# Reordering VectorE and ScalarE work around the fp32 feed-forward matmuls of a two-layer decoder trunk

## The chip, the cores and the metric

The kernel runs on one core of a Trainium2 chip. Its engines are TensorE (PE in the rows, its weight loads PEld), VectorE (DVE), ScalarE (ACT), GpSimd (POOL) and the DMA queue of SyncE (SP). The metric is the device time of one execution in microseconds (us); lower is better. The profile is that of one execution, and "span" is the time from its first to its last instruction.

## The reference

One step of a two-layer decoder trunk over 576 tokens (512 prompt tokens, 64 sample tokens), all in float32. Four SwiGLU feed-forward blocks stand around two mixers:

```python
def rms_norm(x, g):
    xf = x.astype(F32)
    y = xf * lax.rsqrt(jnp.mean(xf * xf, axis=-1, keepdims=True) + EPS)
    return (y * g.astype(F32)).astype(x.dtype)

def swiglu(x, w_gu, w_down):
    g, u = jnp.split(x @ w_gu, 2, axis=-1)
    return (jax.nn.silu(g) * u) @ w_down
...
    for l in range(DEPTH):
        x = x + 0.5 * swiglu(rms_norm(x, ffn1_norm[l]), ffn1_w_gu[l], ffn1_w_down[l])
        h = rms_norm(x, mix_norm[l])
...
        x = x + mix
        x = x + 0.5 * swiglu(rms_norm(x, ffn2_norm[l]), ffn2_w_gu[l], ffn2_w_down[l])
    y = rms_norm(x, final_norm)
```

The model width is 1024 and the hidden width 2816. The mixer of layer 0 is windowed attention with pooling, that of layer 1 a gated width-3 convolution; the change leaves both alone.

## The kernel before, in words

**Numbers.** Every float32 operand of a matmul is split into a high and a low part (`wh`, `wl` for weights; `xh`, `xl`, `exh`, `exl`, `hh`, `hl` for data), and three matmuls (high by high, high by low, low by high) make one product. The high part of a weight is a cast on ACT (L100), the low part a subtraction on DVE (L101). A weight tile has three buffers of each. `W.ahead(n)` issues the splits of the next weight groups, `W.take()` hands out the next one.

**Phases.** FFN 0, attention mixer, FFN 1, FFN 2, convolution, FFN 3, final norm. An FFN goes through the 22 hidden blocks in four chunks of 5, 5, 6 and 6; after a chunk's blocks come its eight down-projections, in the order 0, 4, 1, 5, 2, 6, 3, 7. The last chunk's projections add into x, prepare the next phase's operands from x and add x squared into `sq` (ACT squares into `sqt`, POOL adds, L298).

**A unit.** A hidden block's gate and up product is made with seven block products instead of eight, each a run of 12 matmuls of 128x128 by 128x288 (the tokens are two halves of C = 288). PE issues them in the order B11, T1, B21, T2, B22, T3, and T4 last. They go into three PSUM banks: A (B11, B21: gate of the first half), F (T1, B22: gate of the second half) and B (T2, T3, T4: up). Between them stand copies on ACT: A into B after B11 (L447), F into `p5` after T1 (L472), B into `u2` after T2 (L484). T3 adds to B and so waits for the copy into `u2`; B21 adds to A and waits for the copy of A into B; T4 adds to B and waits until DVE has read B for the *half sum* (h <- B + p5, L399). The gate's first half is multiplied by the norm factor on DVE (L431) and goes through Silu on ACT (L432); the second half is L435, L436, L437.

The weights of a unit are three groups: `a` straight from the loaded tile (`raw`), `e` and `f` from three *weight sums* on DVE (L111 to L113), and `dh`, `dl` for T4. T4 of a unit runs behind B11 of the next (`finish_unit`), because its half sum and split come late. The first unit of a chunk has no unit before it: it runs through the last part of `unit()`, the other units through the part under `if prev:`, which has an order of its own. Of the 16 first units, three (those that begin FFN 1, 2 and 3, `start`) also make the norm factor: column sums of `sq` on PE (L339), a square root on ACT (L343), a refinement on DVE, then transposes on PE (L358), copies into `r` on ACT (L623) and `rm` on DVE. The first three blocks of FFN 0 are done plainly (`first_pairs`), eight products each, while x is still being prepared. The program keeps each engine's order as written; semaphores join the engines.

Of the kernel before, what the change touches and what calls it, by code (L numbers as in the profile page):

```python
# [25 lines left out]
F32 = mybir.dt.float32  # L26
F32R = mybir.dt.float32r
AF = mybir.ActivationFunctionType
ALU = mybir.AluOpType
# [3 lines left out]
C = 288  # L33
# [6 lines left out]
PLAIN = 3  # L40
# [132 lines left out]
class Trunk:  # L173
    def __init__(self, ctx, tc, I, O, phases):
        self.tc, self.nc, self.I, self.O = tc, tc.nc, I, O
        nc = self.nc
# [18 lines left out]
        for ph in phases:  # L195
            if ph[0] == "ffn":
                n = ph[1]
# [4 lines left out]
            elif ph[0] == "ab":  # L202
                g = lambda ap: ap.rearrange("p a b -> p (a b)")
# [6 lines left out]
                units += [(f(I["cvo"][u]), 2048, (1024, 1024)) for u in range(4)]  # L210
        self.W = Weights(nc, self.raw_pool, self.split_pool, units)
        self.phases = phases

    def bank(self, n):
        return self.ps.tile([128, 512], F32, tag=n, name=n, bufs=2 if n == "B" else 3)
# [169 lines left out]
    def seven(self, out, name, w, col, first, last):  # L385
# [3 lines left out]
        for k in range(4):  # L389
            v = slice(col + 128 * k, col + 128 * k + 128)  # L390
            fh, fl = self.form(name, k)
            for z, (a, m) in enumerate(((h, fh), (h, fl), (l, fh))):
                nc.tensor.matmul(out=out, lhsT=a[:, v], rhs=m, start=(first and k == 0 and z == 0),  # L393
                                 stop=(last and k == 3 and z == 2), skip_group_check=True)

    def half_mult(self, s):

        nc, tt = self.nc, self.nc.vector.tensor_tensor
        tt(out=s["h"][:, C:], in0=s["B"][:, :C], in1=s["p5"], op=ALU.add)  # L399
        tt(out=s["h"][:, C:], in0=s["h"][:, C:], in1=s["g"][:, C:], op=ALU.mult)  # L400

    def finish_unit(self, s):

# [12 lines left out]
    def unit(self, u, j, prev, fresh, start, pre, extra=None):  # L416
# [13 lines left out]
        def gate0():  # L430
            tt(out=g0, in0=a, in1=r[:, :C], op=ALU.mult)  # L431
            nc.scalar.activation(out=g0, in_=g0, func=AF.Silu)  # L432
# [15 lines left out]
        if prev:  # L448
# [17 lines left out]
            nc.scalar.activation(out=g1, in_=g1, func=AF.Silu)  # L466
            self.seven(b, "T3", wf, 0, False, False)
            return s
        W.sums(u + 1)
        we = W.take()  # L470
        self.seven(f, "T1", we, 0, True, False)
        nc.scalar.copy(out=s["p5"], in_=f)  # L472
# [1 line left out]
        self.seven(a, "B21", wa, 512, False, True)  # L474
        if not start:
            gate0()
        W.ahead(1)
        if extra:
            extra()
# [9 lines left out]
            ft = self.factor_tiles()  # L489
        else:  # L490
            gate1()
        W.ahead(1)
        self.seven(b, "T3", wf, 0, False, False)
        if start:
            self.factor([fp[j // 4][:, 128 * (j % 4):128 * (j % 4) + v.stop - v.start] for j, v in enumerate(TOKS)], ft)
            gate0()
            gate1()
        return s


# [28 lines left out]
    def first_pairs(self, n):  # L529
        nc, W, tp = self.nc, self.W, self.tp  # L530
        ws = [W.take() for _ in range(2)]
        p0 = [self.pair() for _ in range(2)]
        for k in range(KD):
            for p, w in zip(p0, ws):
                self.eight(p, w, k, 128 * k, k == 0, k == 7)
        sq = [self.sq] + self.sqs
        for i, j in ((0, 1), (2, 3), (0, 2), (4, 5), (6, 7), (4, 6), (0, 4)):
            nc.vector.tensor_tensor(out=sq[i], in0=sq[i], in1=sq[j], op=ALU.add)
        self.hidden_tiles()
        W.ahead(1)  # L540
        for ks in ((0, 1), (2, 3)):
            ts = []
            for k in ks:
                ts.append(tp.tile([128, C], F32, tag="t1", name="t1"))
                nc.vector.tensor_tensor(out=ts[-1], in0=self.x[:, k, :C], in1=self.x[:, k, C:], op=ALU.subtract)
            for k, t in zip(ks, ts):
                self.hi_lo(self.form("T1", k), t, self.gain[:, n, k:k + 1])

        def sums(ks):
            sts = []  # L550
            for k in ks:
                xb = tp.tile([128, C], F32, tag="t1", name="t1")
                nc.scalar.activation(out=xb, in_=self.x[:, k, C:], func=AF.Copy, scale=self.gain[:, n, k:k + 1])
                sts.append((k, xb, tp.tile([128, 3, C], F32, tag="st", name="st")[:, :2]))
            for k, xb, st in sts:
                self.form_t32(k, n, xb, st)
            for k, xb, st in sts:
                self.main_hi(k, st)
            for k, xb, st in sts:
                self.main_lo(k, st)  # L560

        (g0, g1), (u0, u1) = p0
        pg = self.plain(self.pair())
        W.ahead(1)
        outs = [t[:, C:C + 128] for t in (g0, g1, u0, u1)] + [g0[:, 416:480]]
        fa, ft = [], []

        def roots():
            fa.append(self.tok_factor(g1[:, 480:485], (self.sq,), TOKS, later=True))

        def factors():
            self.newton(*fa[0])
            self.factor(outs, self.factor_tiles())

        pu = self.plain((self.bank("B"), self.bank("B")), {1: roots, 5: factors})
        self.plain_out(0, *p0)
        W.ahead(1)
        sums((0, 1))
        p2 = [self.plain(self.pair())]
        self.plain_out(1, pg, pu)  # L580
        W.sums(PLAIN)
        W.ahead(1)
        sums((2, 3))
        p2.append(self.plain(self.pair()))
        W.ahead(1)
        self.plain_out(2, *p2)

    def late_forms(self, n):

# [36 lines left out]
    def ffn(self, i, u0):  # L626
# [4 lines left out]
        for ci, (o, kc) in enumerate(CHUNKS):  # L631
# [17 lines left out]
            held = []  # L649
            for e, d in enumerate(ORDER):  # L650
                if last and kind == "final" and e == 6:
                    self.last_down(kc)
                    break
                w = self.W.next(1 if e == 1 else 2)
                p = self.pair()
                held.append((d, p, w))
                self.down_part(p, w, 0, kc - 1 if e < 2 else kc, kc)
# [4 lines left out]
                if e == 1:  # L662
                    for d, p, w in held:
                        self.down_part(p, w, kc - 1, 1, kc)
                    self.W.ahead(2)
                for d, p, w in held:
                    self.down_out(d, p, last, nxt, kind)
                held = []

    def down_out(self, d, p, last, nxt, kind):  # L670
        nc, tp, tt = self.nc, self.tp, self.nc.vector.tensor_tensor
# [13 lines left out]
            nc.scalar.activation(out=self.xg(d), in_=xd, func=AF.Copy, scale=self.gain[:, 6, d:d + 1])  # L685
        else:
            self.split_x(d, nxt)
        self.square(d, tp)

    def forms(self, d, nxt, tp):  # L690
        if d < 4:
# [899 lines left out]
```

## Time and profile before

| | |
|---|---|
| median of 3 runs | 2321.95 us (2320.99 to 2324.97) |
| the profiled execution's own time | 2320.83 us |
| its span | 2319.0 us |
| PE busy | 2216.7 us, 96% of the span |
| DVE busy | 1627.6 us, 70% |
| ACT busy | 925.3 us, 40% |
| POOL busy | 436.7 us, 19% |
| mean granted TensorE clock | 0.986 |
| share of the DMA engines, loads and stores of SP | 27.8% |

A matmul's busy time is longer than the step from one to the next, since they overlap; the pace is read from their starts. The engines work in parallel, so a busy share alone does not tell what a shorter wait is worth: that is read from PE's pauses and from what ended them.

### The profile page before, as it was taken

To read this page: it belongs to the slowest core of one execution; us is meant where nothing else is said; L and a number is where in the kernel's file an instruction comes from. 1 tells how busy PE (TensorE), PEld (TensorE's weight loads), DVE (VectorE), ACT (ScalarE), POOL (GpSimd) and SP (SyncE) were. 2 spreads that over 40 slices of the span, in tenths; PEclk is the share of its full clock that TensorE was granted. 3 is DMA by queue.
4 is the path that set the end of the run, shared out by engine and by line. 5 is a ranking of instruction groups with operands and counts; after the bars stand their busy time and mean duration, and the time that the engine had idled before them with its cause. 6 is when DMAs were issued, how large, how long until landed. Compare 5 with 4: busy or idle time off the path is not lost. (4 is left out here: it accounts for less than half of the span.)

```text
span 2319.0 us, 39839 instructions
## 1 busy us (share of the span) xinstructions
PE 2216.7 (96%) x16544; PEld 2167.9 (93%) x16544; DVE 1627.6 (70%) x2596; ACT 925.3 (40%) x1604; POOL 436.7 (19%) x444
## 2 busy tenths in 40 slices
PE   8899999999999999999999899999999999999998
PEld 7899999899888899999999899999999999999997
DVE  7586767635666788668587867768664487768584
ACT  5343534323334335344344524344431145335253
POOL 0000101207555640000011101000222211000012
PEclk9899999999999999999999899999999999999999
DMA  3222222443343522222222222322222222222222
GB/s 134 72 77 90 96 87 78 156 140 117 128 140 108 135 87 78 96 83 92 91 76 89 66 84 76 103 91 78 87 93 84 82 70 75 103 82 87 80 98 69
DMA packets 70949, 217.89 MB, mean 94 GB/s; under 512 B 14256, under 2 KB 37808, under 8 KB 54128
## 3 DMA queue, kind: packets, MB, share of 16 engines
q1 hardware_dynamic: 70336, 215.24, 27.8%
q8 instruction: 130, 2.13, 0.4%
q14 instruction: 51, 0.42, 0.1%
q10 hardware_dynamic: 432, 0.10, 0.0%
HBM read 204.22 MB, written 11.10 MB: 93 GB/s over the span
## 5 line engine op out<-in xcount | busy, mean ns | idle before, releaser
L101 DVE TENSOR_TENSOR wl<-raw,wh 128x1024 fp32r<-128x1024 f32 (+3 forms) x305 | 350.7, 1155 | 220.5 <-ACT wh L100 220.3
L100 ACT CAST wh<-raw 128x1024 fp32r<-128x1024 f32 (+3 forms) x305 | 278.1, 914 | 336.6 <-PE F L610 212.3
L414 POOL TENSOR_TENSOR hl<-h,hh 128x576 fp32r<-128x576 f32 x88 | 135.1, 1535 | 1378.8 <-ACT hh L413 1378.8
L393 PE MATMUL B<-xh,wh 128*128 128x288 f32 x680 | 203.1, 299 | 25.8 <-ACT u L484 25.8
L101 DVE TENSOR_TENSOR wl<-sum,wh 128x1024 fp32r<-128x1024 f32 x168 | 206.6, 1230 | 29.6 <-ACT wh L100 29.6
L393 PE MATMUL A<-exh,wh 128*128 128x288 f32 x680 | 204.4, 301 | 7.3 <-ACT B L447 7.1
L100 ACT CAST wh<-sum 128x1024 fp32r<-128x1024 f32 x168 | 174.0, 1047 | 93.4 <-DVE sum L112 92.0
L374 PE MATMUL acc<-xh,wh 128*128 128x288 f32 x960 | 207.7, 298 | 1.7 <-DVE x L681 1.7
L393 PE MATMUL A<-exh,wl 128*128 128x288 f32 x680 | 204.0, 300 | 3.9 <-DVE wl L101 3.9
L374 PE MATMUL acc<-xl,wh 128*128 128x288 f32 x960 | 205.6, 296 | 0.4 <-POOL xl L1441 0.4
L374 PE MATMUL acc<-xh,wl 128*128 128x288 f32 x960 | 205.6, 296 | 0.0
L610 PE MATMUL F<-hh,wh 128*128 128x288 f32 x692 | 205.5, 297 | 0.0
L610 PE MATMUL F<-hl,wh 128*128 128x288 f32 x692 | 205.4, 297 | 0.0
L610 PE MATMUL F<-hh,wl 128*128 128x288 f32 x692 | 205.3, 297 | 0.0
L610 PE MATMUL A<-hh,wl 128*128 128x288 f32 x692 | 204.0, 295 | 1.1 <-DVE wl L101 1.0
L610 PE MATMUL A<-hl,wh 128*128 128x288 f32 x692 | 203.9, 295 | 0.0
L610 PE MATMUL A<-hh,wh 128*128 128x288 f32 x692 | 203.8, 295 | 0.0
L393 PE MATMUL A<-exl,wh 128*128 128x288 f32 x680 | 203.8, 300 | 0.0
L393 PE MATMUL B<-xl,wh 128*128 128x288 f32 x680 | 201.6, 296 | 0.0
L393 PE MATMUL B<-xh,wl 128*128 128x288 f32 x680 | 201.5, 296 | 0.0
L374 PEld LDWEIGHTS acc<-xh,wh 128*128 128x128 f32 x960 | 154.3, 189 | 6.1 <-issue 3.2
L393 PEld LDWEIGHTS B<-xh,wh 128*128 128x128 f32 x680 | 128.9, 189 | 29.2 <-ACT u L484 29.2
(375 smaller groups left out, 6006.8 us busy)
## 6 DMA issues: line engine op xcount, KB each, us to landing
raw<-in_gu SPq DMA_DIRECT2D x87, 1024.0 KB, 4.9
raw<-in_dn SPq DMA_DIRECT2D x32, 768.0 KB, 4.3
raw<-in_dn SPq DMA_DIRECT2D x32, 640.0 KB, 3.9
raw<-in_wqk SPq DMA_DIRECT2D x12, 1024.0 KB, 5.2
raw<-in_cv SPq DMA_DIRECT2D x12, 1024.0 KB, 4.8
kv<-in_kb SPq DMA_DIRECT2D x32, 256.0 KB, 4.2
kv<-in_vb SPq DMA_DIRECT2D x32, 256.0 KB, 4.6
raw<-in_wv SPq DMA_DIRECT2D x6, 1024.0 KB, 4.8
```

The source lines that it names most:

```text
L100: self.nc.scalar.copy(out=h, in_=src)
L101: self.nc.vector.tensor_tensor(out=l, in0=src, in1=h.bitcast(F32), op=ALU.subtract)
L374: nc.tensor.matmul(out=p[:, c, :C], lhsT=w, rhs=m[:, k0 + k, c * C:c * C + C], start=(first and k == 0 and z == 0), stop=(last and k == kn ...
L393: nc.tensor.matmul(out=out, lhsT=a[:, v], rhs=m, start=(first and k == 0 and z == 0), stop=(last and k == 3 and z == 2), skip_group_check= ...
L414: nc.gpsimd.tensor_tensor(out=self.hl[:, j, :], in0=s["h"], in1=self.hh[:, j, :].bitcast(F32), op=ALU.subtract)
L610: nc.tensor.matmul(out=p[c][:, :C], lhsT=a, rhs=m[:, k, c * C:c * C + C], start=(k == 0 and z == 0), stop=(k == kc - 1 and z == 2))
```

## The change

Five orders are written differently; no operation is added or taken away.

1. In a first unit, the weight sums of the next unit (`W.sums(u + 1)`) no longer stand ahead of everything: they come behind the gate product `gate0`, or, in the three units that begin an FFN, behind T3's half sum.
2. The half sum of a first unit comes right behind T3's matmuls, and the split of the next weight group (`W.ahead(1)`) behind it; `half_mult` at the next unit then has nothing left to do.
3. In the units that begin an FFN, the sums and that split stand between the half sum and the copies into `r`.
4. In the last chunk of an FFN, the square of one x block is issued behind the next weight cast.
5. In `first_pairs`, splits of weights are issued earlier, the differences of x halves later, the first sums ahead of the factor copies, and the factor's two steps one k step earlier.

```diff
+    def half_add(self, s):
+
+        if "sum" not in s:
+            s["sum"] = True
+            self.nc.vector.tensor_tensor(out=s["h"][:, C:], in0=s["B"], in1=s["p5"], op=ALU.add)
+
     def half_mult(self, s):
-
-        nc, tt = self.nc, self.nc.vector.tensor_tensor
-        tt(out=s["h"][:, C:], in0=s["B"][:, :C], in1=s["p5"], op=ALU.add)
-        tt(out=s["h"][:, C:], in0=s["h"][:, C:], in1=s["g"][:, C:], op=ALU.mult)
+        self.half_add(s)
+        if "half" not in s:
+            s["half"] = True
+            self.nc.vector.tensor_tensor(out=s["h"][:, C:], in0=s["h"][:, C:], in1=s["g"][:, C:], op=ALU.mult)
...
-        W.sums(u + 1)
         we = W.take()
...
         if not start:
             gate0()
+            W.sums(u + 1)
         W.ahead(1)
...
             gate1()
-        W.ahead(1)
         self.seven(b, "T3", wf, 0, False, False)
+        self.half_add(s)
         if start:
+            W.sums(u + 1)
+            W.ahead(1)
             self.factor([fp[j // 4][:, 128 * (j % 4):128 * (j % 4) + v.stop - v.start] for j, v in enumerate(TOKS)], ft)
             gate0()
             gate1()
+            self.half_mult(s)
+        else:
+            self.half_mult(s)
+            W.ahead(1)
         return s
...
-        W.ahead(1)
-        for ks in ((0, 1), (2, 3)):
...
+        W.ahead(2)
+
+        def differences():
...
         pg = self.plain(self.pair())
-        W.ahead(1)
+        W.ahead(2)
...
         def factors():
             self.newton(*fa[0])
-            self.factor(outs, self.factor_tiles())
-
-        pu = self.plain((self.bank("B"), self.bank("B")), {1: roots, 5: factors})
+            ft = self.factor_tiles()
+            sums((0, 1))
+            self.factor(outs, ft)
+
+        pu = self.plain((self.bank("B"), self.bank("B")), {0: roots, 4: factors})
+        W.ahead(1)
         self.plain_out(0, *p0)
-        W.ahead(1)
-        sums((0, 1))
+        differences()
         p2 = [self.plain(self.pair())]
+        W.sums(PLAIN)
         self.plain_out(1, pg, pu)
-        W.sums(PLAIN)
-        W.ahead(1)
+        W.ahead(2)
         sums((2, 3))
         p2.append(self.plain(self.pair()))
+        self.plain_out(2, *p2)
         W.ahead(1)
-        self.plain_out(2, *p2)
...
                 w = self.W.next(1 if e == 1 else 2)
+                if self.late_square:
+                    self.late_square()
+                    self.late_square = None
                 p = self.pair()
...
-        self.square(d, tp)
+        self.late_square = lambda: self.square(d, tp)
```

PE's order differs at the two factor steps of `first_pairs` alone, and the orders of POOL and SP are the same in both programs. Three places of the other two engines follow.

DVE, first unit of the second chunk of FFN 0 (a first unit that begins no FFN); `wl<-sum` are the groups e and f, `wl<-raw` is the next unit's group a. Before:

```order
L101 TENSOR_TENSOR wl<-sum,wh 128x1024
L111 TENSOR_TENSOR sum<-raw 128x1024
L112 TENSOR_TENSOR sum<-sum,raw 128x512
L113 TENSOR_TENSOR sum<-sum,raw 128x512
L101 TENSOR_TENSOR dl<-raw,dh 128x512
L431 TENSOR_TENSOR g<-A,r 128x288
L101 TENSOR_TENSOR wl<-raw,wh 128x1024
L435 TENSOR_TENSOR g<-F,u_1231 128x288
L436 TENSOR_TENSOR g<-g,r 128x288
L101 TENSOR_TENSOR wl<-sum,wh 128x1024
L399 TENSOR_TENSOR h<-B,p_1230 128x288
L400 TENSOR_TENSOR h<-h,g 128x288
```

The same stretch of DVE in the changed program:

```order
L101 TENSOR_TENSOR wl<-sum,wh 128x1024
L101 TENSOR_TENSOR dl<-raw,dh 128x512
L438 TENSOR_TENSOR g<-A,r 128x288
L111 TENSOR_TENSOR sum<-raw 128x1024
L112 TENSOR_TENSOR sum<-sum,raw 128x512
L113 TENSOR_TENSOR sum<-sum,raw 128x512
L101 TENSOR_TENSOR wl<-raw,wh 128x1024
L442 TENSOR_TENSOR g<-F,u_1231 128x288
L443 TENSOR_TENSOR g<-g,r 128x288
L401 TENSOR_TENSOR h<-B,p_1230 128x288
L407 TENSOR_TENSOR h<-h,g 128x288
L101 TENSOR_TENSOR wl<-sum,wh 128x1024 x2
```

The three sums moved from ahead of `dl` to behind the gate product, and the half sum (L399, now L401) from behind a split to ahead of it; ACT's order there is the same in both.

DVE, the unit that begins FFN 3, from the split `dl` on (`fr` are the steps of the norm factor, `ft` its widened tiles). Before:

```order
L101 TENSOR_TENSOR dl<-raw,dh 128x512
L101 TENSOR_TENSOR wl<-raw,wh 128x1024
L342 TENSOR_SCALAR fr<-F 128x5
L313 RECIPROCAL fr<-fr 128x5
L314 TENSOR_TENSOR fr<-fr 128x5
L315 SCALAR_TENSOR_TENSOR fr<-fr 128x5
L316 SCALAR_TENSOR_TENSOR fr<-fr 128x5
L353 TENSOR_SCALAR ft<-ones,fr 128x128 x4
L353 TENSOR_SCALAR ft<-ones,fr 64x128
L101 TENSOR_TENSOR wl<-sum,wh 128x1024
L624 TENSOR_SCALAR rm<-r 128x576
L431 TENSOR_TENSOR g<-A,r 128x288
```

In the changed program, from the widened tiles on:

```order
L354 TENSOR_SCALAR ft<-ones,fr 128x128 x4
L354 TENSOR_SCALAR ft<-ones,fr 64x128
L401 TENSOR_TENSOR h<-B,p_19556 128x288
L111 TENSOR_TENSOR sum<-raw 128x1024
L112 TENSOR_TENSOR sum<-sum,raw 128x512
L113 TENSOR_TENSOR sum<-sum,raw 128x512
L101 TENSOR_TENSOR wl<-sum,wh 128x1024
L641 TENSOR_SCALAR rm<-r 128x576
L438 TENSOR_TENSOR g<-A,r 128x288
```

The sums, which stood ahead of `dl`, now stand behind the half sum, which waits for T3's last matmul, and ahead of the split of group e. On ACT the cast of that group (`wh<-sum`) stands ahead of the copies into `r` in both programs.

ACT, the last chunk of FFN 1, rounds of d = 1, 5 (`exh`, `xh` prepare the next FFN's operands, `sqt` is the square). Before:

```order
L243 ACTIVATE exh<-t_12958,gain 128x288
L255 ACTIVATE xb<-x,gain 128x288
L297 ACTIVATE sqt<-x 128x576
L100 CAST wh<-raw 128x768
L243 ACTIVATE exh<-x,gain 128x288
L243 ACTIVATE xh<-x,gain 128x288
L284 CAST xh<-st 128x864
L297 ACTIVATE sqt<-x 128x576
L100 CAST wh<-raw 128x768
```

In the changed program:

```order
L244 ACTIVATE exh<-t_12958,gain 128x288
L256 ACTIVATE xb<-x,gain 128x288
L100 CAST wh<-raw 128x768
L298 ACTIVATE sqt<-x 128x576
L244 ACTIVATE exh<-x,gain 128x288
L244 ACTIVATE xh<-x,gain 128x288
L285 CAST xh<-st 128x864
L100 CAST wh<-raw 128x768
L298 ACTIVATE sqt<-x 128x576
```

Each square changed places with the weight cast behind it.

## Rows read from the trace of the kernel before

**Rows 1.** The page, part 1: busy us (share of span) x instructions.

```profile
PE 2216.7 (96%) x16544; PEld 2167.9 (93%) x16544; DVE 1627.6 (70%) x2596; ACT 925.3 (40%) x1604; POOL 436.7 (19%) x444
```

**Rows 2.** Waits of PE, whole span: total us, times, longest us.

```profile
PE B L393 <- ACT u L484: 25.8, 15, 5.1
PE B L393 <- DVE h L399: 18.8, 14, 1.4
...
PE F L393 <- ACT wh L100: 4.5, 2, 3.7
```

**Rows 3.** Timeline of PE, FFN 0's second chunk: start, length, what [idle before].

```profile
127.86 0.29 PE L393 MATMUL B<-xh,wh 128*128 128x288 f32 x1
...
132.88 0.40 PE L393 MATMUL B<-xh,wh 128*128 128x288 f32 x1 [1.70 <-ACT u L484]
...
137.75 0.40 PE L393 MATMUL B<-xh,dh 128*128 128x288 f32 x1 [1.41 <-DVE h L399]
...
139.45 0.29 PE L393 MATMUL A<-exh,wh 128*128 128x288 f32 x1
...
147.41 0.30 PE L393 MATMUL A<-exh,wh 128*128 128x288 f32 x1
```

**Rows 4.** Timeline of DVE, the same first unit.

```profile
127.47 1.23 DVE L111 TENSOR_TENSOR sum<-raw 128x1024 f32<-128x1024 f32 x1
...
130.07 0.69 DVE L101 TENSOR_TENSOR dl<-raw,dh 128x512 fp32r<-128x512 f32 x1
130.67 0.45 DVE L431 TENSOR_TENSOR g<-A,r 128x288 f32<-128x288 f32 x1
132.56 1.23 DVE L101 TENSOR_TENSOR wl<-raw,wh 128x1024 fp32r<-128x1024 f32 x1 [1.44 <-ACT wh L100]
...
137.24 0.45 DVE L399 TENSOR_TENSOR h<-B,p 128x288 f32<-128x288 f32 x1
```

**Rows 5.** Timeline of ACT, the same first unit.

```profile
131.15 0.44 ACT L432 ACTIVATE g<-g 128x288 f32<-128x288 f32 x1 [3.77 <-DVE g L431]
...
132.44 0.39 ACT L484 COPY u<-B 128x288 f32<-128x288 f32 x1
134.68 0.45 ACT L437 ACTIVATE g<-g 128x288 f32<-128x288 f32 x1 [1.86 <-DVE g L436]
...
136.92 0.39 ACT L447 COPY B<-A 128x288 f32<-128x288 f32 x1
```

**Rows 6.** Timeline of PE, first unit of FFN 0's last chunk.

```profile
332.95 0.40 PE L393 MATMUL B<-xh,wh 128*128 128x288 f32 x1 [1.18 <-ACT u L484]
```

**Rows 7.** Windows: length, busy us (count) of PE, PEld, DVE, ACT, POOL; PEclk, DMA, GB/s.

```profile
146.50:157.70 11.20, 11.20 (x87) 11.20 (x86) 9.94 (x14) 6.20 (x10) 1.44 (x1) 1.00 0.28 94
347.00:358.50 11.50, 11.45 (x86) 11.21 (x86) 10.91 (x15) 6.10 (x10) 1.95 (x1) 1.00 0.27 93
864.64:868.05 3.41, 3.41 (x15) 3.41 (x16) 3.34 (x4) 2.85 (x4) 2.92 (x2) 0.50 0.00 0
25.70:62.80 37.10, 31.65 (x208) 29.90 (x208) 27.47 (x52) 19.96 (x34) 4.47 (x3) 0.86 0.16 58
```

**Rows 8.** Timeline of ACT, the unit that begins FFN 3.

```profile
1913.70 0.77 ACT L623 COPY r<-A 128x128 f32<-128x128 f32 x4 [1.45 <-PE A L358]
...
1914.60 1.28 ACT L432 ACT_TABLE_LOAD   x1
...
1917.62 0.39 ACT L447 COPY B<-A 128x288 f32<-128x288 f32 x1
```

**Rows 9.** Timeline of PE, the unit that begins FFN 3 and the next.

```profile
1911.35 0.40 PE L393 MATMUL B<-xh,wh 128*128 128x288 f32 x1 [0.34 <-ACT u L484]
...
1918.43 0.29 PE L393 MATMUL A<-exh,wh 128*128 128x288 f32 x1
```

**Rows 10.** Timeline of POOL and DVE, last chunk of FFN 1.

```profile
1256.80 1.43 POOL L298 TENSOR_TENSOR sq<-sq,sqt 128x576 f32<-128x576 f32 x1 [2.03 <-ACT sqt L297]
1257.41 1.63 DVE L101 TENSOR_TENSOR wl<-raw,wh 128x768 fp32r<-128x768 f32 x1 [1.21 <-ACT wh L100]
```

More of the change, by code (lines that the diff above doesn't have):

```diff
@@ L539, in first_pairs @@
         self.hidden_tiles()
-        W.ahead(1)
-        for ks in ((0, 1), (2, 3)):
[L542 to L547, printed above, removed]
+        W.ahead(2)
+        def differences():
+            for ks in ((0, 1), (2, 3)):
+                ts = []
+                for k in ks:
+                    ts.append(tp.tile([128, C], F32, tag="t1", name="t1"))
+                    nc.vector.tensor_tensor(out=ts[-1], in0=self.x[:, k, :C], in1=self.x[:, k, C:], op=ALU.subtract)
+                for k, t in zip(ks, ts):
+                    self.hi_lo(self.form("T1", k), t, self.gain[:, n, k:k + 1])
         def sums(ks):
@@ L563, in first_pairs @@
         pg = self.plain(self.pair())
-        W.ahead(1)
+        W.ahead(2)
         outs = [t[:, C:C + 128] for t in (g0, g1, u0, u1)] + [g0[:, 416:480]]
-        fa, ft = [], []
+        fa = []
         def roots():
@@ L654, in ffn @@
                 w = self.W.next(1 if e == 1 else 2)
+                if self.late_square:
+                    self.late_square()
+                    self.late_square = None
                 p = self.pair()
@@ L666, in ffn @@
                 for d, p, w in held:
+                    if self.late_square:
+                        self.late_square()
                     self.down_out(d, p, last, nxt, kind)
                 held = []
+            if self.late_square and kind != "final":
+                self.late_square()
+                self.late_square = None
     def down_out(self, d, p, last, nxt, kind):
```

## Prediction

> **What bounds the kernel now.** I read the page's busy times first. PE is busy for 2216.7 of 2319.0 us and DVE for 1627.6 [rows 1]: PE is the bound, and no reordering of other engines can give back more than its 102.3 us of pauses, plus what a low clock costs behind some of them. Next I read the waits of PE, to see which pauses there are. Two stand out [rows 2]: T3 waits for the copy of B into `u2` (25.8 us in 15 times, one of 5.1 in the first unit of FFN 0) and T4 for the half sum (18.8 us in 14 times). Then I read the three engines' timelines where these happen, the first unit of a chunk. The reader is to see that PE is not short of data there but of one small operation that stands late in another engine's order. Last come the windows, for how full DVE is in a plain unit and what the clock does behind a pause.
>
> **Ordinary first units (12 of 16).** The cost of a first unit's two waits: from T2 at 127.86 to the next unit's B21 at 139.45 PE issues five groups (T2, B22, T3, B11, T4) in 11.59 us; the five groups from that B21 to the following B11 at 147.41 take 7.96, or 1.59 each [rows 3]. The waits cost 3.63 us, more than the 1.70 + 1.41 shown, because overlap is lost too. In the last chunk of an FFN the first wait is 1.18 [rows 6], so the cost is 3.11. Eight units at 3.63 and four at 3.11 make 41.5 us.
>
> Does the new order remove both? Step by step in rows 3 to 5. Without the sums, `dl` takes the place of the first at 127.47 and ends at 128.2; the gate product needs B21, whose last matmul ends about then (T2 starts at 127.86), so it ends near 128.6 and not at 131.1. From the start of Silu to the end of the copy into `u2` ACT took 132.83 - 131.15 = 1.68, so the copy ends at 130.3. T3's turn is at 127.86 + 2 x 1.59 = 131.04: 0.7 us to spare, the T3 wait goes.
>
> Next could be late what now stands behind the sums. They took 130.07 - 127.47 = 2.6 us, so they end near 131.15 and the split of the next `a` (1.23) at 132.4. B11's turn is 132.63, and its third matmul, the first to read a low part, comes about 0.27 later: 0.5 to spare. Silu of the second half stood 2.12 us behind the start of that split (132.56 to 134.68), so it starts at 133.2. The half sum needs T3's end (about 132.8) and DVE, which is past the second gate product at 133.1; it ends near 133.6, where T4's turn is 134.22. The T4 wait goes, 0.6 to spare.
>
> The next thing late is the copy of A into B, at the end of ACT's queue behind two casts. From Silu's start it took 137.31 - 134.68 = 2.63, so it ends at 135.85, and B21's turn is 135.81. That is a tie; I allow 0.1 us, and 0.4 as the bound.
>
> One limit more. A plain unit has DVE busy for 9.94 of 11.2 us, but a last chunk's unit, which has one more product, for 10.91 of 11.5 [rows 7]. DVE has next to no slack there, so units that follow can be earlier only by what DVE is: its gate product moves from 130.67 to about 128.1, so I count 2.5 for these four and 3.53 for the eight. **Sum: 8 x 3.53 + 4 x 2.5 = 38.2 us gained.** With the copy at its bound and 0.4 more lost to DVE in each unit, it is 8 x 2.8 + 4 x 2.0 = 30.4.
>
> **The three units that begin an FFN.** Here the order turns against the kernel. The sums leave the path ahead of the square root, which helps T3 where it waited (0.34 us in FFN 3 [rows 9]; more in FFN 1). But they now stand behind the half sum, so behind T3's end, and the cast of group e, which needs them, stands on ACT ahead of the copies into `r`; those stand ahead of the table load, both Silus, a cast and the copy of A into B. B21 of the next unit waits for that copy. In FFN 3 T3 would start at about 1910.85 and end 1.75 later, at 1912.6. Then: half sum 0.5 (with its start), the first two sums 1.23 + 0.72 and a cast 1.1 (the four as in a first unit [rows 4, 5]), copies 1914.60 - 1913.70 = 0.9, and from the table load to the end of the copy into B 1918.01 - 1914.60 = 3.41 [rows 8]: 7.9 us. DVE's path is some 0.4 longer, since the split of e (1.23) stands ahead of `rm`. So B21 comes at 1912.6 + 8.3 = 1920.9, not at 1918.43 [rows 9]: **2.4 lost in FFN 3.** In FFN 1 the chain loses the same 2.4, but T3's wait there is longer and shrinks; the sums' 2.6 us bound that, I take half: **1.1 lost**. In both, PE's next groups are done early (transposes, B11 and T4, some 4.2 us), so PE stands for about 4 us ahead of B21, once each.
>
> What such a pause does to the clock: behind the pause at the end of the attention mixer the window from 864.64 on has PE busy all its 3.41 us at a granted clock of 0.50, the lower of its two levels, 1.2 GHz [rows 7]. Half of that is lost, 1.7 us. I charge it once in each of the three units: **5.1 lost.** The bounds are nothing and twice that.
>
> The Trainium skill (ScalarE: Activation LUTs, section "What ACT_TABLE_LOAD costs") adds a drain of about 1.38 us to each load of a different table set, some 2.66 in all. Here the load took 1.28, beginning 1914.60, and the chain that I use runs straight through it [rows 8]; by the page three such chains would be 1.4 longer each and the forecast 4 us higher. The row decides.
>
> **Squares behind the cast, last chunks.** In FFN 1's last chunk POOL's addition began at 1256.80 and DVE's split of a 768-wide weight at 1257.41; the split took 1.63 and ended 0.81 after the addition did [rows 10]. By the 1.23 us of a 1024-wide split [rows 4] it needs about 0.95, so it lost 0.7 to POOL. With the square behind the cast, the cast starts earlier by a square's length on ACT (between the 0.44 of a Silu on half as many columns [rows 5] and twice that; I take 0.65; DVE had waited 1.21 for this cast), and the split is under way when POOL starts. Five such rounds are worth up to 5 x 1.35 = 6.8 us on DVE's path at the end of FFN 1, where PE waits for casts and splits (3.7 in one wait for the cast of e [rows 2]). I take 5 of them as reaching B21 of FFN 2's first unit; its new chain behind T3 is 8.3 where it was about 5.3 (T3's end at 1913.1 to B21 at 1918.43 in FFN 3 [rows 9]), so 3.0 go back, and for less time at the low clock I count half of 1.7: **2.8 gained at the start of FFN 2**, bounds 0 and 6. At the ends of FFN 0 and FFN 2 only the last split counts, because PE does not wait before: 0.65 each, **1.3 gained**. In FFN 3 it changes nothing on the path, since the same casts come in time.
>
> **First pairs.** DVE was idle for 9.6 of the 37.1 us from 25.70 to 62.80, and PE's clock was 0.86 there [rows 7]. The new order moves eight differences (four casts on ACT) behind the first product and the weight splits forward; it adds no work. Going through it with the same durations, DVE comes to the last pair's split some 1.5 us earlier and ACT to the copy into `u2`, T3's longest wait [rows 2], 1.9 earlier (both estimates): the pieces are the same, and the unit behind still waits for its late forms. Two things are worse: the copies into `r` stand behind two more casts on ACT, so the third pair's bank comes free 0.7 later, and the first split of the unit comes behind the second pair's product, so B11 pauses a little over 1 us. **1.9 gained**, bounds 5 gained and 3 lost.
>
> **At no cost.** The new tests in `half_mult` are Python alone. SP's order is unchanged: no load is moved past another; they only start up to 2.6 earlier, at a DMA share of 0.28 in a unit [rows 7].
>
> **Sum.** 38.2 - 2.4 - 1.1 - 5.1 + 2.8 + 1.3 + 1.9 = 35.6 us. The profiled execution took 2320.83, so 2285.2; the median of the runs shown is 1.1 above it, so **2286 us** as a median. A difference under 0.2% (4.6 us) could not be told from no change.
>
> **Rivals.**
> - *DVE becomes the bound in every chunk.* For: 0.5 to 0.7 us of slack in each step, and a tie at B21. Against: 1.26 us idle per plain unit [rows 7]. Then each first unit gives 2.5 as in a last chunk, 30 in all, and the starts pay the low clock twice (5.1 more): 2286 + 8 + 5 = 2299. Chance 0.17.
> - *The starts are mild and the first pairs better.* The clock stays up behind the new pauses (5.1 back) and the first pairs take their bound (3.1 more): 2278, and 2274 if FFN 2's start gives all it can. Chance 0.17.
> - *T3 is held by something else than the gate product.* Then only the T4 wait goes, 12 x 1.6 = 19 us, less the starts: 2307. Against: T3's releaser is the copy in all 15 cases, and the copy follows Silu at once. Chance 0.03.
> - *Slower: the wait only moves to the copy of A into B.* Its place is ACT, where two casts stand ahead of it. It decides if that copy comes 3.2 us later than reckoned, because a cast then waits for a weight buffer or for sums that POOL slows: 12 x 3.2 more gives 2324. Against: the buffers' last readers (T2, T3) end before the casts' turn. Chance 0.03.
>
> My forecast has 0.58, and 0.02 are left for small losses in many places that bring it within 0.2%. A range from 2273 to 2299 leaves out about 2 in 10: it holds the bounds of the ordinary units (30.4 and 41.5 gained) with the starts either way. Faster 0.95, within 0.2% 0.02, slower 0.03.
>
> **What the profile would show.** Right: T3's wait for the copy into `u2` gone in the 12 ordinary units, T4's for the half sum gone in all, a new wait of B21 for the copy from A near 4 us in each of the three units that begin an FFN, with a stretch of 1.2 GHz behind it; splits in FFN 1's last chunk near 0.95 and not 1.63. Wrong: B21 waiting in ordinary units by more than 0.4, T4 waiting in the third unit of a chunk, or no pause at the three starts.

## The result, and the profile after

The three executions of the changed kernel took 2287.83 (the profiled one), 2294.12 and 2295.74 us beside a median of 2323.46 for the kernel before: ratio 0.9867 (95% interval 0.985 to 0.9884). A fourth execution took 4300.34 us, nearly twice as long, is left out of the ratio and has no explanation here. A later repeat (below) gave 2295.49 and 0.9882 (0.9869 to 0.9894). So the kernel is faster by 1.2 to 1.3%, some 29 us. The forecast was 2286 with a range from 2273 to 2299: sign and range were right; the usual execution lies 8 to 9 us above the forecast, the profiled one 2.6 above what was forecast for it (2285.2).

The page of the changed kernel, part 1, answers to [rows 1]:

```profile
PE 2214.1 (97%) x16544; PEld 2168.9 (95%) x16544; DVE 1614.8 (71%) x2596; ACT 925.7 (40%) x1604; POOL 441.0 (19%) x444
```

PE does the same work in a span of 2286.0 us: its pauses fell from 102.3 to 71.9 us. Where they went is in the waits of PE (total us, times, longest), beside [rows 2]:

```profile
PE A L394 <- ACT B L454: 22.6, 6, 5.7
...
PE B L394 <- ACT u L491: 4.9, 2, 4.1
...
PE F L394 <- ACT wh L100: 3.2, 1, 3.2
...
PE B L394 <- DVE h L401: 0.7, 4, 0.2
```

The two large waits are as good as gone: 25.8 us in 15 times became 4.9 in 2, 18.8 in 14 became 0.7 in 4. A third has grown: B21 waiting for the copy of A into B, 7.1 us in 4 times before, is 22.6 in 6: 11.8 in three new pauses at the starts of FFN 1, 2 and 3, 5.7 in the first unit of FFN 0 and 5.0 in two waits that stood there before (4.7).

The ordinary first unit of [rows 3 to 5], now: timeline of PE, the first matmuls of T2, T3, T4, B21 and the following B11, and then T4 of the third unit.

```profile
125.90 0.30 PE L394 MATMUL B<-xh,wh 128*128 128x288 f32 x1
...
129.06 0.30 PE L394 MATMUL B<-xh,wh 128*128 128x288 f32 x1
...
132.25 0.29 PE L394 MATMUL B<-xh,dh 128*128 128x288 f32 x1
...
133.86 0.40 PE L394 MATMUL A<-exh,wh 128*128 128x288 f32 x1
...
141.92 0.30 PE L394 MATMUL A<-exh,wh 128*128 128x288 f32 x1
...
143.69 0.40 PE L394 MATMUL B<-xh,dh 128*128 128x288 f32 x1
```

T2 to B21 takes 7.96 us, five groups at 1.59 with no pause; it was 11.59. The timelines of DVE and POOL there, and under them that of ACT:

```profile
126.10 0.46 DVE L438 TENSOR_TENSOR g<-A,r 128x288 f32<-128x288 f32 x1
126.47 1.22 DVE L111 TENSOR_TENSOR sum<-raw 128x1024 f32<-128x1024 f32 x1
...
131.06 0.46 DVE L401 TENSOR_TENSOR h<-B,p 128x288 f32<-128x288 f32 x1
...
136.16 1.44 POOL L421 TENSOR_TENSOR hl<-h,hh 128x576 fp32r<-128x576 f32 x1 [41.24 <-ACT hh L420]
136.21 2.48 DVE L111 TENSOR_TENSOR sum<-raw 128x1024 f32<-128x1024 f32 x1
```

```profile
126.59 0.45 ACT L439 ACTIVATE g<-g 128x288 f32<-128x288 f32 x1 [1.16 <-DVE g L438]
...
127.88 0.39 ACT L491 COPY u<-B 128x288 f32<-128x288 f32 x1
...
133.41 0.40 ACT L454 COPY B<-A 128x288 f32<-128x288 f32 x1
```

The gate product stands ahead of the sums, so the copy into `u2` ends at 128.27 and T3 goes on at 129.06 with 0.8 to spare (forecast 0.7). The half sum ends at 131.52, T4's turn is 132.25 (0.7 to spare, forecast 0.6). The copy of A into B ends at 133.81 and B21 starts at 133.86: the tie that was forecast. One small new loss shows in the third unit: the sums for it begin just behind the start of an operation of POOL and the first of them takes 2.48 instead of 1.22 us, the half sum behind them is late, and T4 at 143.69 loses 0.17.

The other side of the change, the unit that begins FFN 3 [rows 8, 9]: timelines of PE, DVE and ACT.

```profile
1892.84 0.42 PE L394 MATMUL A<-exh,wh 128*128 128x288 f32 x1 [3.89 <-ACT B L454]
...
1884.83 0.46 DVE L401 TENSOR_TENSOR h<-B,p 128x288 f32<-128x288 f32 x1 [0.97 <-PE B L394]
1885.20 1.22 DVE L111 TENSOR_TENSOR sum<-raw 128x1024 f32<-128x1024 f32 x1
...
1887.18 1.05 ACT L100 CAST wh<-sum 128x1024 fp32r<-128x1024 f32 x1 [5.02 <-DVE sum L112]
1888.13 0.76 ACT L640 COPY r<-A 128x128 f32<-128x128 f32 x4
...
1889.02 1.28 ACT L439 ACT_TABLE_LOAD   x1
1890.32 0.44 ACT L439 ACTIVATE g<-g 128x288 f32<-128x288 f32 x1
...
1892.39 0.39 ACT L454 COPY B<-A 128x288 f32<-128x288 f32 x1
```

From T3's end, where the half sum starts (1884.83), to B21 pass 8.0 us; the forecast's chain was 8.3. Each link is the one named: half sum, sums, a cast that waits 5.02 us for them, copies into `r`, table load, both Silus, a cast, the copy. The page of the Trainium skill that the prediction weighed (ScalarE: Activation LUTs, section "What ACT_TABLE_LOAD costs") would add a drain of 1.38 us to the load; here the load starts 0.02 us behind the end of the copies and Silu 0.02 us behind the end of the load, so the row decides.

The other two pauses, ahead of B21 in the units behind the starts of FFN 1 and FFN 2, in the timeline of PE:

```profile
876.40 0.61 PE L394 MATMUL A<-exh,wh 128*128 128x288 f32 x1 [3.90 <-ACT B L454]
...
1285.12 0.40 PE L394 MATMUL A<-exh,wh 128*128 128x288 f32 x1 [4.02 <-ACT B L454]
```

Last the windows (length; busy us and count of PE, PEld, DVE, ACT, POOL; granted clock, DMA share, GB/s), beside [rows 7]: behind the pauses at the starts of FFN 3, 1 and 2, then a plain unit.

```profile
1893.08:1896.49 3.41, 3.41 (x16) 3.41 (x16) 2.19 (x5) 0.99 (x3) 1.42 (x1) 0.50 0.29 43
875.91:879.32 3.41, 2.92 (x12) 2.93 (x13) 2.19 (x3) 1.65 (x4) 0.80 (x1) 0.50 0.13 14
1285.51:1288.92 3.41, 3.41 (x17) 3.41 (x16) 2.30 (x5) 1.10 (x3) 1.41 (x1) 0.50 0.30 46
...
146.50:157.70 11.20, 11.20 (x86) 11.20 (x86) 9.95 (x14) 6.24 (x11) 1.44 (x1) 1.00 0.27 95
```

Behind each of the three pauses PE runs at the lower of its two levels, 1.2 GHz. DVE's load in a plain unit is what it was.

### The profile page after: what moved, and what is told of

Same layout as the page of the kernel before. It is cut to its first block, busy times and chain, and to the rows that moved or that the text cites. A ratio compares the mean times of both kernels' runs of the same rounds, so it can differ in the third digit from the quotient of the medians.

```text
span 2286.0 us, 39851 instructions
## 1 busy us (share of the span) xinstructions
PE 2214.1 (97%) x16544; PEld 2168.9 (95%) x16544; DVE 1614.8 (71%) x2596; ACT 925.7 (40%) x1604; POOL 441.0 (19%) x444
## 4 chain that ended last, share of the span: by engine, by line
PE 56%; DVE 6%; ACT 1%; issue 1%; POOL 0%; POOLq 0%; ACTq 0%; DVEq 0%
PE B L394 12%; PE acc L375 10%; PE F L627 8%; PE A L627 8%; PE F L394 8%; PE A L394 8%; DVE wl L101 1%; ACT wh L100 1%; DVE sum L112 1%; DVE sum L111 1%; DVE x L707 0%; DVE sum L113 0%; DVE dl L101 0%; DVE xl L289 0%; PE A L751 0%
## 5 line engine op out<-in xcount | busy, mean ns | idle before, releaser
L101 DVE TENSOR_TENSOR wl<-raw,wh 128x1024 fp32r<-128x1024 f32 (+3 forms) x305 | 339.8, 1119 | 196.4 <-ACT wh L100 195.6
L394 PE MATMUL A<-exh,wh 128*128 128x288 f32 x680 | 206.9, 304 | 22.9 <-ACT B L454 22.6
L101 DVE TENSOR_TENSOR wl<-sum,wh 128x1024 fp32r<-128x1024 f32 x168 | 205.7, 1231 | 17.5 <-ACT wh L100 17.5
L394 PEld LDWEIGHTS A<-exh,wh 128*128 128x128 f32 x680 | 131.4, 193 | 25.6 <-ACT B L454 24.1
```

The lines of the kernel that those rows point to most:

```text
L101: self.nc.vector.tensor_tensor(out=l, in0=src, in1=h.bitcast(F32), op=ALU.subtract)
```

## The experiments

Each run has four to six executions. The runs stand in three groups, each on one chip with its own runs of the kernel before (medians 2323.56, 2324.23, 2322.07); comparisons between groups go by the ratios.

**A repeat, and its clock.** The changed kernel once more, unaltered. Expected:

> The changed kernel once more, for its spread. Theory: 2288 to 2296 us, 1.2 to 1.5% faster than before, and in its profile three pauses of PE of 3.9 us ahead of B21, one in each unit that begins an FFN, each with a stretch of 1.2 GHz behind it; the spread between executions comes from how long those stretches are. Rival: the spread has nothing to do with the clock, and the granted clock is the same in fast and slower executions.

Measured: 2295.49 us (2291.91 to 2297.31). The cores' view (span, mean granted clock) of this profile, and under it that of the first one:

```profile
core 0: 2295.5 us, clock 0.982
```

```profile
core 0: 2286.0 us, clock 0.986
```

With two levels, 1 and 0.5, a mean of 0.982 is 2 x 0.018 x 2295.5 = 83 us at the lower one, and 0.986 is 64. Half of the 19 us between them would be 9.3, and the spans differ by 9.5. Compared matmul by matmul, the repeat loses about 5.6 of the 9.5 us at four places where it has a stretch at the lower clock that the first profile lacks or has shorter (near 11, 73, 588 and 865 us), and another 2.1 between 770 and 800 us, where the stretches are equally long. So the clock makes most of the difference, not all of it. Across the seven executions of the changed kernel in both groups time goes with the clock, from 2287.8 at 0.986 to 2297.3 at 0.982. The mean of their clocks is 0.9834; over the eleven executions of the kernel before in this group it is 0.9854. So the first profile, with a clock like that of before, is not the usual case.

**The three starts in the old order.** In the units that begin an FFN, sums, split and half sum stand as before; all else is as changed.

```diff
+        if start:
+            W.sums(u + 1)
         we = W.take()
...
+        if start:
+            W.ahead(1)
         self.seven(b, "T3", wf, 0, False, False)
-        self.half_add(s)
+        if not start:
+            self.half_add(s)
         if start:
-            W.sums(u + 1)
-            W.ahead(1)
```

Expected:

> The changed kernel with the three units that begin an FFN in their old order. Theory (the new order costs there 2 to 4 us each, and a stretch at the low clock): the three pauses of 3.9 us are gone, the old waits of T3 (2.1 in FFN 1, 0.3 in FFN 3) and T4 (about 1) are back, and the time is 8 to 11 us below the changed kernel, near 2283. Rival (the new order only moves the old waits there): within 3 us of the changed kernel, or above it.

Measured: 2279.03 us, ratio 0.9811 (0.9798 to 0.9824), mean clock 0.987. The same kernel was run once more in the third group. Expected:

> A repeat of the changed kernel with the three starts in the old order, beside the other two, to see how far its median moves: 2277 to 2281 by the earlier one, if the 16 us between it and the changed kernel belong to the starts; 2283 or more if a part of them was the clock of that execution alone.

Measured: 2277.67 us, again 0.9811 (0.9797 to 0.9824). Timeline of PE around the start of FFN 3 (T3, T4, B21):

```profile
1876.96 0.40 PE L394 MATMUL B<-xh,wh 128*128 128x288 f32 x1 [0.34 <-ACT u L493]
...
1882.33 0.40 PE L394 MATMUL B<-xh,dh 128*128 128x288 f32 x1 [0.94 <-DVE h L401]
1884.04 0.29 PE L394 MATMUL A<-exh,wh 128*128 128x288 f32 x1
```

The pause ahead of B21 is gone, the two small waits of before are back. Starts compared group by group: the three pauses put B21 back by 3.9 to 4.1 each, 12.0 together; T3 and T4 take 6.0 back; the waits of the new order cost 6.0 net, where the forecast had 2.4 + 1.1 + 3.0 = 6.5. By unit it is 0.1 to 0.6 in FFN 1 (1.1 forecast), 3.0 in FFN 2 (3.0) and 2.6 in FFN 3 (2.4). The whole difference is 0.0071 of 2323, 16.5 us (4 either way). Most of the rest goes with the clock: 0.9834 to 0.987 is 76 to 59 us at the lower level, or 8 to 9 us if half of that time is lost. So the new order of the starts is a loss, as forecast, and larger than the 10.75 charged for it (the 6.5, and 4.25 for the clock).

**The starts alone.** The kernel before with only the new order of the starts (the same edit the other way round). Expected:

> The kernel before with the new order in the three units that begin an FFN alone. Theory: three pauses of about 4 us ahead of B21 appear, and the time is 6 to 12 us above before, near 2331. Rival: T3's and T4's waits that go there pay for the pauses, and the time is within 3 us of before.

Measured: 2335.64 us, ratio 1.0058 (1.0045 to 1.0071), 13.5 us slower, mean clock 0.982. It agrees from the other side: at its three starts B21 comes 3.94, 4.07 and 3.94 later by the pauses, and the time at the lower level grows by 17 us.

**The pauses filled.** The changed kernel, with 20 matmuls that nobody reads ahead of B21 in the unit behind a start; PE stands idle there anyway.

```diff
+            if prev["start"]:
+                self.fill(f, wa, 20)
             self.seven(a, "B21", wa, 512, False, True)
```

Expected:

> The changed kernel with 20 matmuls of 288 columns that nobody reads (2.7 us at full clock) issued in each of the three pauses ahead of B21, in front of that group. Theory (PE's standing idle is what brings the low clock behind these pauses): the pauses end as late as before but show as waits of about 1.2 instead of 3.9 us, the stretches of 3.41 us at 0.50 behind them are gone, and with 3 x 1.7 us the kernel takes about 2290, 5 below the changed one (2295). Rival (the clock falls there for another reason, or the added work is itself slow): the stretches stay or move, no gain, 2294 to 2298.

Measured: 2285.12 us, ratio 0.9841 (0.9828 to 0.9855), mean clock 0.9875. The windows behind the same three B21 groups:

```profile
1888.33:1891.74 3.41, 3.41 (x25) 3.41 (x26) 3.39 (x5) 2.19 (x4) 1.30 (x1) 1.00 0.25 41
875.51:878.92 3.41, 3.41 (x25) 3.41 (x26) 3.38 (x5) 2.19 (x4) 1.28 (x1) 1.00 0.32 43
1282.11:1285.52 3.41, 3.41 (x25) 3.41 (x26) 3.40 (x5) 2.20 (x4) 1.35 (x1) 1.00 0.30 38
```

The clock stays at 2.4 GHz in all three, with 25 matmuls in 3.41 us instead of 12 to 17, and the groups behind start 1.3 to 1.5 us earlier each time. That the idle pause brings the low clock is thus shown. By the traces it costs 4.3 us at the three places, where 5.1 were charged (the two profiled spans differ by 5.5); by the ratios the filled kernel gains 9.5 (4 either way). What the timed executions gained beyond that was not found at the three pauses.

**The pauses left in the old starts, filled too.** Added to the kernel with the old starts: in FFN 2's first unit 21 idle matmuls ahead of T1 and 17 ahead of B21, in FFN 1's and FFN 3's 8 and 5 ahead of B21.

```diff
+            self.fill(f, wa, {2: 0, 3: 21, 5: 0}[self.fi])
         we = W.take()
         self.seven(f, "T1", we, 0, True, False)
...
+            self.fill(fp[0][:, :C], wa, {2: 8, 3: 17, 5: 5}[self.fi])
         self.seven(a, "B21", wa, 512, False, True)
```

Expected:

> The kernel with the three starts in the old order (2279), with matmuls that nobody reads in the pauses that are left in the first unit of FFN 1 (8 ahead of B21), FFN 2 (21 ahead of T1, 17 ahead of B21) and FFN 3 (5 ahead of B21). Theory (idle time brings the low clock): the stretch of 13.65 us at 0.50 at the start of FFN 2 shrinks to 3.4 to 6.8 and the kernel takes 2274 to 2276. Rival (the clock is low there for another reason, so the added matmuls run at half speed and end behind the wait that they should fill): the stretch stays and the kernel takes 2279 to 2284.

Measured: 2278.91 us, ratio 0.9813 (0.9799 to 0.9826): no gain that shows, though the mean clock rose to 0.99. Stretches of 3.4 us at the lower clock stay at the starts of FFN 1 and FFN 3; the one at FFN 2's start is gone. The window of FFN 2's start, from B11's first matmul with a low part to B22, in this kernel, and under it in the kernel with the old starts:

```profile
1258.42:1273.22 14.80, 12.03 (x88) 11.31 (x88) 13.38 (x18) 9.01 (x14) 3.46 (x2) 1.00 0.00 1
```

```profile
1254.53:1271.80 17.27, 11.02 (x50) 10.06 (x50) 14.99 (x19) 9.02 (x14) 3.43 (x2) 0.60 0.05 9
```

The same work (50 matmuls, and 38 idle ones) at the full clock instead of 0.60 takes 2.5 us less, of which T3's wait behind it takes 0.6 back. A mean of 0.60 is 13.8 us at the lower level, so half of it would have been 6.9. But DVE is busy for 13.38 of 14.80 us here, and PE waits for it and for casts at either level. The unfilled kernel's own second profile has a shorter stretch there (10.2 us and not 13.7) and is 1.1 us earlier at that start without any filling. The theory was right on the clock and wrong on its worth: here most of the time at the lower level fell where PE had to wait anyway. What is left, 1.9 us, is less than these timings tell apart.

**Sums ahead again.** The changed kernel with the weight sums back at the head of the 13 ordinary first units; the early half sum stays.

```diff
+        if not start:
+            W.sums(u + 1)
         we = W.take()
...
-            W.sums(u + 1)
```

Expected:

> The changed kernel with the weight sums back ahead of the gate product in the 12 ordinary first units, the half sum still early. Theory (two waits that add up): T3's waits of 1.7 and 1.2 us for the copy into u2 are back, T4's are not, and the time is 8 x 1.86 + 4 x 1.33 = 20 us above the changed kernel, near 2313. Rival (DVE sets the pace behind the first unit, so one of the two steps gives most of the gain): at most 10 us above the changed kernel.

Measured: 2308.66 us, ratio 0.9938 (0.9925 to 0.995): 13 us lost, between the two. PE's waits:

```profile
PE B L394 <- ACT u L492: 24.8, 14, 5.6
...
PE B L394 <- DVE h L401: 0.7, 4, 0.2
```

T3's wait is back, T4's is not. Start by start, T3 comes 1.86 to 1.88 later in a unit of the eight and 1.34 in one of the last chunks, and about 0.3 of that comes back by the end of the chunk: 8 x 1.6 + 4 x 1.05 = 17 us. The time shows 4 less; the clock (0.9846 beside 0.9834) may account for up to 3 of that. The two moves thus share the gain about evenly: the sums' place gives T3's wait, the half sum's place T4's.

**Squares as before.** Each square stands again ahead of the next weight cast.

```diff
-                    self.late_square()
...
-        self.late_square = lambda: self.square(d, tp)
+        self.square(d, tp)
```

Expected:

> The changed kernel with one part undone: each square of the norms stands again ahead of the next weight cast on ACT. Theory (the lock between DVE and POOL and the square's own length both count at the ends of FFN 0, 1 and 2): splits in FFN 1's last chunk near 1.63 us again, the wait of T1 for the cast of e at FFN 2's start some 4 us longer, the waits at the ends of FFN 0 and FFN 2 back from 0.88 to 1.65: 4 to 6 us above the changed kernel (2295 in its repeat). Rival (the squares cost only their own place at the two tails, and the gain at FFN 2's start came from elsewhere): 0 to 2 us above it.

Measured: 2298.49 us, ratio 0.9899 (0.988 to 0.9919), 4 us above the repeat, but the two intervals overlap; the traces have to decide. The splits in FFN 1's last chunk (group of L101 on DVE, 1228 to 1258 us: duration min/median/max), first in the changed kernel, then here:

```profile
L101 DVE TENSOR_TENSOR wl<-raw,wh x4: 951/960/1222, 1237.6 to 1253.2; 128x768 fp32r<-128x768 f32 x3, 128x1024 fp32r<-128x1024 f32 x1
```

```profile
L101 DVE TENSOR_TENSOR wl<-raw,wh x5: 951/1633/1854, 1229.2 to 1253.5; 128x768 fp32r<-128x768 f32 x5
```

0.96 against 1.63 us, as forecast (0.95). At FFN 2's start B11 comes 2.0 later and T1 another 2.6: 4.6 us, where the prediction took 5. PE's wait for the last block of x at the ends of FFN 0 and FFN 2 is 1.7 us each here and 0.9 each in the changed kernel (1.7 and 1.6 before): 1.5 gained in all, where the prediction had 1.3.

**First pairs as before.** The old order of the first three pairs. The edit puts back the old lines of the diff, of which these are the core:

```diff
-        W.ahead(2)
-        def differences():
...
+        W.ahead(1)
+        for ks in ((0, 1), (2, 3)):
...
-        pu = self.plain((self.bank("B"), self.bank("B")), {0: roots, 4: factors})
+        pu = self.plain((self.bank("B"), self.bank("B")), {1: roots, 5: factors})
```

Expected:

> The changed kernel with the first three pairs in the old order. Theory: T3's wait in FFN 0's first unit back to 5.1 from 4.1 us, T1's too, the pause of 5.7 ahead of B21 there back to about 4: 1 to 3 us above the changed kernel. Rival (the new order only moves the wait from T3 to B21 there): no difference, within 1 us.

Measured: 2294.42 us, ratio 0.9876 (0.9859 to 0.9893): no difference. Timeline of PE from 50 to 80 us, the larger waits alone, in the changed kernel and then here:

```profile
50.39 0.40 PE L394 MATMUL A<-exh,wh 128*128 128x288 f32 x1 [0.29 <-ACT wh L100]
...
52.02 0.40 PE L394 MATMUL A<-exh,wl 128*128 128x288 f32 x1 [1.10 <-DVE wl L101]
...
60.93 0.61 PE L394 MATMUL A<-exh,wh 128*128 128x288 f32 x1 [5.73 <-ACT B L454]
...
72.75 0.40 PE L394 MATMUL B<-xh,wh 128*128 128x288 f32 x1 [4.10 <-ACT u L491]
```

```profile
52.02 0.40 PE L394 MATMUL A<-exh,wl 128*128 128x288 f32 x1 [2.52 <-DVE wl L101]
55.64 0.61 PE L394 MATMUL F<-exh,wh 128*128 128x288 f32 x1 [2.03 <-ACT wh L100]
...
61.22 0.61 PE L394 MATMUL A<-exh,wh 128*128 128x288 f32 x1 [1.55 <-ACT B L454]
...
73.04 0.61 PE L394 MATMUL B<-xh,wh 128*128 128x288 f32 x1 [5.40 <-ACT u L491]
```

Of the waits in B11 and ahead of T1 the new order leaves 1.4 us of 4.6, and it makes the one ahead of B21 5.73 instead of 1.55; T3 starts 0.29 us apart. The rival is right that the wait only moves; it moved from T1 to B21, and T3's is no measure of it (4.10 and 5.40 here, 5.42 in the repeat's profile with the new order).

**Two other orders for the starts.** First, sums and split as before, but the half sum right behind T3 and its product behind the gates:

```diff
+        if start:
+            W.sums(u + 1)
         we = W.take()
...
+        if start:
+            W.ahead(1)
         self.seven(b, "T3", wf, 0, False, False)
         self.half_add(s)
         if start:
-            W.sums(u + 1)
-            W.ahead(1)
```

Expected:

> The changed kernel with two of the three moves undone in the units that begin an FFN: weight sums and the next split stand ahead of T3's half sum as in the old order, but the half sum itself stands right behind T3 and only its product with the gate stays behind the gates. Theory (the pause ahead of B21 comes from the sums and the split that stand between T3 and the copies into r, not from the half sum): no pause of 3.9 us ahead of B21 in these units, T3's wait of about 2.1 for the copy into u2 there as in the old order, T4's wait of 0.9 for the half sum gone: 2276 to 2279, so 0 to 3 below the kernel with all three starts in the old order (2279) and 16 to 19 below the changed one. Rival (the half sum's wait for T3 holds up DVE, and with it the factor and the chain to the copy): B21 pauses by 1 to 2 us, 2279 to 2284.

Measured: 2281.38 us, ratio 0.9820 (0.9803 to 0.9837). Timeline of PE at FFN 3's B21:

```profile
1887.16 0.40 PE L394 MATMUL A<-exh,wh 128*128 128x288 f32 x1 [0.68 <-ACT B L454]
```

The pauses of 3.9 are 0.26, 0.69 and 0.68, so it was the sums and the split that made them, not the half sum. T4's wait is gone, but two thirds of it stand now ahead of B21 at FFN 2 and 3; from the old starts' 2279 and 2278 the time can't be told apart.

Second, the copy of A into B ahead of the next group's cast in every unit that follows another, with the starts' sums early and their split behind the gates:

```diff
         self.seven(a, "B11", wa, 0, True, False)
-        W.ahead(1)
+        if not prev:
+            W.ahead(1)
         nc.scalar.copy(out=b, in_=a)
         if prev:
+            W.ahead(1)
```

Expected:

> The changed kernel with the copy of A into B put ahead of the cast of the next group in every unit that follows a first unit, and in the units that begin an FFN the sums ahead of T3's half sum and the split behind the gates. Theory (B21 waits for a copy that stands at the end of ACT's queue behind two casts): the pauses of 3.9 us ahead of B21 shrink to 1 to 2 or go, T1 of the unit behind may wait for its cast by up to 0.5 instead: 2276 to 2284, 10 to 18 below the changed kernel. Rival (the chain through the square root alone holds the copy): the pauses stay above 3 us, and 2290 to 2297.

Measured: 2293.07 us, ratio 0.9871 (0.9855 to 0.9888), no better than the changed kernel, though its pauses are 1.2 to 1.4. PE's waits tell why:

```profile
PE B L394 <- DVE h L401: 8.9, 38, 0.6
...
PE F L394 <- ACT p L468: 2.1, 7, 0.3
```

The later cast makes the split, and with it the half sum, late in 38 units, where the changed kernel has four such waits. Neither theory had this.

## Why the prediction was right or wrong

**What bounds the kernel: right.** PE's busy time is unchanged, and what was gained are its pauses.

**Ordinary first units: right, 2 us too high.** Forecast 38.2. By the starts of the groups, T3 comes 1.86 and T4 another 1.58 earlier in each of the eight, B21 behind them the full 3.53 or a little more, as forecast; then 0.17 goes back in the third unit of seven of them, and some 0.1 behind it. The four last chunks give 2.5, as forecast, so DVE's lack of slack there was read rightly. Seven of the eight units end up 3.25 earlier, the eighth 3.41; with 4 x 2.5 that is 36.2. The 0.17 is the sign that the prediction listed as "T4 waiting in the third unit". Its cause is in the rows above: the first of the sums for that unit starts 0.05 us behind an operation of POOL and takes twice its time (1.85 in that place before). The shape of it, waiting until POOL's end (137.60) and then running whole (to 138.69), is what the Trainium skill (SBUF — State Buffer, section "SBUF: two separate sides") calls an exclusive lock on a shared port pair; the trace agrees. In the kernel before, too, all 37 such sums that begin during an operation of POOL end 1.08 us behind its end, however early in it they began. In the one chunk of the eight where POOL starts later than the sum (FFN 2's third, at 1465.50), the sum takes 1.22 and T4 loses 0.02.

**The starts: mechanism right, the clock mis-sized.** The waits cost 6.0 us (6.5 forecast). "I charge it once in each of the three units: 5.1 lost" is near what the three stretches at 1.2 GHz cost, 4.3, as the filled pauses show. But the timed executions lose more: 16.5 and 13.5 us for the whole order, 9.5 for the clock alone, each about 4 either way. The prediction's bound of twice 5.1 just holds that.

**From the profiled execution to the median: the step that failed.** The prediction added 1.1 us, the distance of the kernel before. In the changed kernel it is about 7, since most executions run at 0.982 to 0.985 and the profiled one at 0.986. In the first profile the forecast's 35.6 us were 33.0, and the terms as the traces show them come near that: 36.2 - 6.0 - 4.3 + 4.6 + 1.5 + 0.3 = 32.3. The median shows 29. So the sum holds for the first profile as a whole, and the forecast of the usual time is off because it carries over the kernel before's distance, while the usual execution of the changed kernel spends more of its time at the lower clock (mean 0.9834, before 0.9854).

**Squares: right.** 4.6 us for the 5 taken at FFN 2's start, 1.5 for the 1.3 at the ends of FFN 0 and FFN 2. The gain there was then eaten by the start's own order: about 1.0 lost where 1.1 gained was the sum with the clock.

**First pairs: wrong.** The 1.9 gained is 0.3 in the trace and nothing in the time; "B11 pauses a little over 1 us" was right (1.10), but B21 behind it waits 5.73, which the prediction did not have. That the next chunk starts 2.0 us earlier than before in the first profile, close to the 1.9, is luck: in the repeat's profile it starts 0.6 later than before.

**The rivals.** DVE is no new bound (9.95 of 11.2 us busy in a plain unit); its forecast of 2299 was too high, though at 2294 to 2295.5 the time lies nearer to it than to 2286; and the mild starts' 2278 was too low. Neither T3's releaser nor the copy of A into B in ordinary units was misread.

**Open:** why the low clock also shows more often or longer far from the three pauses. The repeat has two stretches that the first profile lacks, near 11 and 588 us, and longer ones near 73 and 865. Of these only the last lies in a unit that the change of the starts touches, and the second profile of the kernel with the old starts has those near 11 and 588 too. No run here tells that apart. A larger supply of buffers, which would take the sums off the starts' path in another way, was not tried.

**A better version.** The changed kernel with the three starts in the old order takes 2278 to 2279 us, 0.9811 of before: some 16 us less than the change as it was made.

## What to carry to other kernels

Move a small operation ahead only after following the longest chain that it then stands in: here much the same move gave 2.5 to 3.3 us in each of twelve units and lost 6 us in three, because in those the chain to the next unit's B21 passed through it. In this kernel a pause of 3.9 us on TensorE cost its length and then some 1.4 us by the clock behind it; matmuls that nobody reads kept the clock there, but they paid only where real work followed at once. Where a kernel's executions differ by more than the effect, compare their mean clocks before you compare their times.

## What the runs showed that was not expected

- Two executions of the same program differed by 9.5 us in span, most of it by the clock (mean 0.986 and 0.982).
- With 38 idle matmuls the granted clock at FFN 2's start rose from 0.60 to 1.00, and the stretch became 2.5 us shorter, not 6.9.
- A 1024-wide addition on DVE that begins 0.05 us behind an operation of POOL took 2.48 instead of 1.22 us; in the kernel before, each of the 37 that began during one ended 1.08 us behind its end.
